# RWKV-7 scan of a diffusion trunk: its main loop laid out by hand over four units instead of by the scheduler's priorities

## The chip, the cores and the metric

One core of one Trainium2 chip runs the whole program, in fp32. The metric is the time of one execution in device microseconds (us), and lower is better.

## The reference

The program is a trunk of two layers over 512 latent tokens and 256 context tokens of width 1024. Each layer is half a SwiGLU, a token mixer, and half a SwiGLU; layer 0 mixes with HGRN2, layer 1 with RWKV-7. Only the scan of RWKV-7 is touched. Per head (16 of width 64) and per direction it computes

```python
def step(s, inp):
    dec, kt, vt, kkt, bt = inp[:5]
    sa = jnp.einsum('bhvk,bhk->bhv', s, kkt)
    s = s * dec[:, :, None, :] - sa[..., None] * bt[:, :, None, :] + vt[..., None] * kt[:, :, None, :]
    y = jnp.einsum('bhvk,bhk->bhv', s, inp[5]) if with_out else None
    return s, y
```

once over the context, whose final state starts the latent scan, and then over the latents, forward and backward; the two outputs are added, normed per head, gated and projected.

## The kernel before

The scan (`rwkv_scan`) works in chunks of 64 tokens. Twelve units (`todo`) are done one after the other: four groups of four heads (`qd`), and in each one unit of context (`g` = 0) and two of latents (`g` = 1, 2). A unit holds both directions (`d`), two head pairs (`e`), two heads to a pair (`hp`) and four chunks (`c`). Its steps, each a generator that yields between pieces:

- `prep_a`: loads hw, KR and ld (lines 1247, 1258, 1261) through SP's queue; decays on TensorE and ACT (sw, cum; tiles sg, E, Ei); scaled keys KR and BK on DVE (lines 1295, 1298); the products A on TensorE (line 1321) and their masked copies N and Ar on DVE (line 1327); the transpose NT (line 1332); and 16 small stores of 16x16 blocks, eight of N and eight of NT, to the DRAM tensor md (line 1335).
- `prep_m`: loads md as M (line 1347) and inverts all blocks on POOL in 14 pairs of small operations (lines 1353, 1354), then stores M to the DRAM tensor me (line 1357, from POOL's queue).
- `prep_d`: 16 small loads of me into X (line 1368).
- `prep_b`: loads VU (line 1377); turns BK into BKT (`bkt`, evicted by ACT at line 1386); products kT and W into KW.
- `prep_c`: transposes X on DVE (line 1409), merges the 16-blocks to 32 and 64 (T16, t16, R16, A32, AT32, TT, Yo, Y: lines 1421 to 1462), then four products YK (line 1472) whose evictions write KW and VU (lines 1473 to 1478), and four products P whose evictions write KR (lines 1486 to 1493).
- `scan`: four steps of the state G (lines 1519 to 1525) and, for latents, two outputs y (lines 1535 to 1545).
- `readout`: norm and gate of a head group's output, after its third unit.

The main loop takes one unit per turn. It emits the scan of unit i with pieces of the inversions, of the preparation of unit i+1 (`prep_b`, `prep_c`, `prep_d`) and of `prep_a` of unit i+2, at rates `RM`, `RP` and `RO`; the scheduler then orders each engine's and each queue's instructions by its own estimate of time, with a raised priority for three of the generators (`urgent`, `HP`). So the order on TensorE, DVE, ACT, POOL and SP is what the scheduler made of it. The PSUM banks of tags "a" (A, sw, cum) and "b" (bkt, kT, W, T16, R16, TT, Yo, YK, P) are two each, and X, VU, M, md and me have two buffers each.

Of the kernel before, what the change touches and what calls it, by code (L numbers as in the profile page):

```python
# [9 lines left out]
F32 = mybir.dt.float32  # L10
# [3 lines left out]
ALU = mybir.AluOpType  # L14
# [12 lines left out]
RINGS, NQ2, NG = {"KR": 6, "BK": 3, "Ar": 4}, 10, 5  # L27
# [44 lines left out]
def trunk(ctx, tc, io, phases=None, dump=None):  # L72
# [1109 lines left out]
    def rwkv_scan(l):  # L1182
# [11 lines left out]
        def Q(name):  # L1194
            if name not in RINGS:
                if "B2" in late:
                    if name == "N":
                        return late["B2"].tile([128, 1024], F32, tag="N", name=name, bufs=4)
                    return late["B2"].tile([128, 1024], F32, tag="Q", name=name, bufs=NQ2)
                ring = "Ar" if name == "N" else "KR"  # L1200
            else:
                ring = name
            return B1.tile([128, 1024], F32, tag=ring, name=name, bufs=RINGS[ring])
# [36 lines left out]
        def prep_a(qd, g):  # L1240
# [8 lines left out]
            gt = B1.tile([128, 4, 4], F32, tag="gt", name="gt", bufs=3)  # L1249
            gs = decays[qd, g] = B1.tile([128, 4], F32, tag="gs", name="gs", bufs=3)  # L1250
            lds, sgs, EEs = [], [], []
            for d in range(2):
                t0 = starts(g)[d]
                kr = Q("KR")[:, :1024]
# [4 lines left out]
                ld = B1.tile([128, 2, 2, 256], F32, tag="L", name="ld", bufs=2)  # L1259
# [52 lines left out]
            for d in range(2):  # L1312
# [4 lines left out]
                for e in range(2):  # L1317
                    for hp in range(2):
                        p = bank("A", "a")
                        for c in range(4):  # L1320
                            pe.matmul(p[:, 128 * c:128 * c + cols], BK[d][half(hp), 4 * e + c].rearrange("p s n -> p (s n)"),  # L1321
                                      KR[d][half(hp), 4 * e + c][:, :1 + lat], start=True, stop=True)
                        pv = p.rearrange("p (c s n) -> p c s n", s=2, n=64)
# [5 lines left out]
                        yield  # L1329
# [10 lines left out]
        def prep_m(qd, g):  # L1340
# [6 lines left out]
            nc.sync.dma_start(out=M, in_=md)  # L1347
# [13 lines left out]
        def prep_d(qd, g):  # L1361
            while (qd, g) not in inverse:
                yield
# [6 lines left out]
        def prep_b(qd, g):  # L1370
            KR, BK, N, Ar, gt, _ = ready[qd, g]
            BKT = [None, None]
            VU = late["B2"].tile([128, 2, 4, 2, 2, 64], F32, tag="VU", name="VU", bufs=2)
            for d in range(2):
                t0 = starts(g)[d]
                for hp in range(2):
                    nc.sync.dma_start(out=VU[half(1 - hp), d, :, hp].rearrange("p c e n -> p c (e n)"),
                                      in_=S["v"][t0:t0 + 256, hp, 128 * qd:128 * qd + 128].rearrange("(c p) n -> p c n", p=64))

            for d in range(2):  # L1380
# [7 lines left out]

            KW = [Q("KW").rearrange("p (e c x n) -> p e c x n", e=2, c=4, x=2) for _ in range(2)]
            for d in range(2):  # L1390
# [10 lines left out]
            ready[qd, g] = KR, N, Ar, BKT, VU, KW, gt  # L1401

        def prep_c(qd, g):
# [14 lines left out]
            for d in range(2):  # L1418
# [3 lines left out]
                yield  # L1422
            dve.tensor_tensor(t16.rearrange("p d s n -> p (d s) n"), p.rearrange("p d s n -> p (d s) n"), off16.unsqueeze(1).to_broadcast([128, 16, 32]), ALU.mult)
            p = view(bank("R16"))
            for d in range(2):
# [3 lines left out]
                yield  # L1429
# [9 lines left out]
            for stage in range(2):  # L1439
                for c in range(8):  # L1440
# [9 lines left out]
                    if c % 4 == 3:  # L1450
                        yield
                if stage == 0:
                    act.activation(tt, pt[:, :256], AF.Copy)
            for d in range(2):
# [46 lines left out]
        def scan(qd, g, KR, Ar, BKT, VU, gt):  # L1501
# [10 lines left out]
            for i in range(4):  # L1512
# [14 lines left out]
                if lat and i % 2:  # L1527

                    p = bank("y", "s")
                    pv = p.rearrange("p (q d e n) -> p q d e n", q=2, d=2, e=2)  # L1530
                    two = [(q, d, e, hp) for q in range(2) for d, e in DE for hp in range(2)]
                    where = lambda q, d: (i - 1 + q, q) if d == 0 else (4 - i - 1 + 1 - q, 1 - q)
                    for n, (q, d, e, hp) in enumerate(two):
                        c, o = where(q, d)
                        pe.matmul(pv[half(hp), o, d, e], VU[:, d, c, hp, e], Ar[d][:, slot(hp, e, c)], start=n < 2, stop=True, skip_group_check=n > 1)
                    for n, (q, d, e, hp) in enumerate(two):
                        c, o = where(q, d)
                        pe.matmul(pv[half(hp), o, d, e], Gs[i - 1 + q][half(hp), 2 * d + e], KR[d][half(hp), 4 * e + c, 1], start=False, stop=True, skip_group_check=True)
                    for d in range(2):
                        t0 = starts(g)[d] + 64 * where(0 if d == 0 else 1, d)[0]  # L1540
                        dst = yb[:, :, t0:t0 + 128].rearrange("p e (q n) -> p q e n", q=2)
                        if g == 1:
                            act.activation(dst, pv[:, :, d], AF.Copy)
                        else:
                            dve.tensor_tensor(dst, dst, pv[:, :, d], ALU.add)
                    yield
            state["G"] = G
# [44 lines left out]
        none = out = iter(())  # L1592
        stage = lambda f, i: f(*todo[i]) if i < len(todo) else none
        second = prep_a(*todo[1])

        def prologue():
            yield from prep_a(*todo[0])
            yield from both(prep_m(*todo[0]), islice(second, NPRO))
# [5 lines left out]
        for _ in both(second, chain(prep_d(*todo[0]), prep_b(*todo[0]), prep_c(*todo[0]))):  # L1604
            pass
        inversions = chain(*(prep_m(*k) for k in todo[1:]))
        third = stage(prep_a, 2)
        next(third)
        for i, k in enumerate(todo):
            ahead, third = urgent(third, HP[1]), stage(prep_a, i + 3)  # L1610
            b, c, d = stage(prep_b, i + 1), urgent(stage(prep_c, i + 1), HP[2]), urgent(stage(prep_d, i + 1), HP[2])
            prep = chain(islice(third, 1), islice(ahead, 4), b, d, ahead, c)
            due = [0.0] * 3
            for _ in urgent(scan(*k, *ready.pop(k)), HP[0]):
                for n, (f, r) in enumerate(((inversions, RM), (prep, RP), (out, RO))):
                    due[n] += r
                    while due[n] >= 1.0:
                        due[n] -= 1.0
                        next(f, None)
            for _ in prep:  # L1620
                next(inversions, None)
# [194 lines left out]
```

## Time and profile before

| | us |
|---|---|
| median of 3 runs (4023.62 to 4033.61) | 4023.75 |
| the profiled execution | 4034.11 |
| its span | 4032.3 |
| TensorE busy in the span | 3604.5 |
| DVE busy | 2515.7 |
| from the first whole X (unit 1) to the last (unit 11) | 619.95 |
| TensorE busy in that stretch | 475.54 |

Busy times are unions of an engine's instructions. TensorE's are modelled from pipelined records, and an fp32 product appears as two records. "PEclk" is the granted clock of TensorE as a share of 2.4 GHz. An idle time names what ended it. The scan's loop runs from about 2860 to 3557 us of the span.

### The profile page before, as it was taken

What the parts mean: (1) busy time and instruction counts of PE and PEld (TensorE: products, weight loads), DVE (VectorE), ACT (ScalarE), POOL (GpSimd) and SP (SyncE); (2) the same over time, 40 slices, a digit from 0 to 9 for tenths busy, and PEclk for the clock granted to TensorE, in tenths of its full rate; (3) what the DMA queues carried; (4) which work ended last, traced back from release to release, by engine and by line L of the source; (5) the groups of instructions that cost most, each with busy time, mean ns of one, the idle gap of its engine ahead of it and who ended that gap; (6) DMA issues with size and microseconds to landing.
All of it is one profiled execution on the core that took longest, in us unless ns stands there. A gap on an engine that the chain in (4) does not pass through costs nothing.

```text
span 4032.3 us, 71742 instructions
## 1 busy us (share of the span) xinstructions
PE 3604.5 (89%) x29954; PEld 3178.6 (79%) x29954; DVE 2515.7 (62%) x4108; ACT 1346.4 (33%) x2080; POOL 1073.7 (27%) x999
## 2 busy tenths in 40 slices
PE   5999997999997999998999997899777877788998
PEld 3899996788885888887999985667666766677887
DVE  6666767556667766657766666673333434268886
ACT  4333333333233333224332333443212222234343
POOL 3222224333344321214212214321101111014332
PEclk9999998999998999998999998998877878788999
DMA  5332321311112334332232232466212212132332
GB/s 186 115 95 89 108 71 48 110 43 43 43 43 63 92 104 124 100 100 68 89 98 80 83 96 65 132 227 186 72 48 53 72 46 61 32 110 72 96 95 83
DMA packets 520546, 356.90 MB, mean 89 GB/s; under 512 B 86589, under 2 KB 494941, under 8 KB 520222
## 3 DMA queue, kind: packets, MB, share of 16 engines
q1 hardware_dynamic: 518494, 348.65, 28.8%
q8 instruction: 235, 3.85, 0.4%
q10 hardware_dynamic: 1152, 2.10, 0.2%
q0 software_dynamic: 576, 1.57, 0.1%
q14 instruction: 89, 0.73, 0.1%
HBM read 312.52 MB, written 39.72 MB: 87 GB/s over the span
## 4 chain that ended last, share of the span: by engine, by line
PE 35%; DVE 6%; DMA 3%; POOL 2%; SPq 2%; issue 2%; ACT 1%; DVEq 0%; POOLq 0%; ACTq 0%
PE po L605 8%; PE c L532 6%; PE a L532 4%; PE b L532 3%; PE k L220 2%; PE v L220 1%; PE bkt L293 1%; SPq L1368 1%; PE A L1321 1%; POOL M L1354 1%; POOL mt L1353 1%; SPq L1335 1%; PE YK L1472 1%; PE G L1519 1%; DMA M<-md 1%
## 5 line engine op out<-in xcount | busy, mean ns | idle before, releaser
L605 PE MATMUL po<-g,whi 128*128 128x512 f32 (+1 forms) x2464 | 593.3, 350 | 10.2 <-ACT g L209 10.2
L532 PE MATMUL c<-u,whi 128*128 128x386 f32 (+1 forms) x2112 | 524.1, 332 | 50.8 <-DVE uu L563 15.9
L524 ACT ACTIVATE whi<-raw 128x1024 fp32r<-128x1024 f32 x352 | 332.8, 950 | 571.8 <-PE po L605 314.2
L549 POOL TENSOR_TENSOR raw<-raw 128x512 f32<-128x512 f32 x88 | 124.1, 1410 | 1374.1 <-DMA raw<-in_ffn_w_in 1040.3
L605 PEld LDWEIGHTS po<-g,whi 128*128 128x128 f32 x2464 | 406.3, 190 | 84.6 <-issue 11.4
L525 DVE TENSOR_TENSOR wlo<-raw,whi 128x1024 fp32r<-128x1024 f32 x352 | 412.1, 1174 | 33.7 <-ACT whi L524 31.9
L532 PEld LDWEIGHTS c<-u,whi 128*128 128x128 f32 x2112 | 371.2, 191 | 78.4 <-ACT u L444 30.1
L532 PE MATMUL a<-u,whi 128*128 128x386 f32 (+1 forms) x1408 | 350.1, 333 | 22.8 <-DVE u L426 17.2
L605 PE MATMUL po<-g,wlo 128*128 128x512 f32 (+1 forms) x1232 | 367.0, 348 | 0.0
L609 DVE SCALAR_TENSOR_TENSOR h<-po,mod,h 128x512 f32<-128x512 f32 (+1 forms) x384 | 228.3, 628 | 194.3 <-PE po L605 194.2
L532 PE MATMUL b<-u,whi 128*128 128x386 f32 (+1 forms) x1408 | 343.4, 328 | 2.6 <-DVE u L447 1.4
L532 PE MATMUL c<-u,wlo 128*128 128x386 f32 (+1 forms) x1056 | 344.8, 327 | 0.0
L532 PEld LDWEIGHTS a<-u,whi 128*128 128x128 f32 x1408 | 254.2, 194 | 28.5 <-issue 18.4
L194 ACT ACTIVATE whi<-raw 128x1024 fp32r<-128x1024 f32 (+1 forms) x193 | 184.5, 959 | 264.4 <-PE c L532 108.5
L532 PEld LDWEIGHTS b<-u,whi 128*128 128x128 f32 x1408 | 246.0, 189 | 12.6 <-issue 6.6
L532 PE MATMUL a<-u,wlo 128*128 128x386 f32 (+1 forms) x704 | 234.2, 333 | 0.2 <-DVE wlo L525 0.2
L605 PEld LDWEIGHTS po<-g,wlo 128*128 128x128 f32 x1232 | 207.9, 190 | 29.8
L532 PE MATMUL b<-u,wlo 128*128 128x386 f32 (+1 forms) x704 | 229.1, 325 | 0.7 <-DVE wlo L525 0.7
L1353 POOL TENSOR_TENSOR mt<-M 128x14 f32<-128x14 f32 (+6 forms) x168 | 44.6, 265 | 644.8 <-DMA M<-md 632.6
L195 POOL TENSOR_TENSOR wlo<-raw,whi 128x1024 fp32r<-128x1024 f32 x48 | 127.1, 2650 | 301.0 <-ACT whi L194 273.0
L532 PEld LDWEIGHTS c<-u,wlo 128*128 128x128 f32 x1056 | 203.3, 193 | 0.0
L195 DVE TENSOR_TENSOR wlo<-raw,whi 128x768 fp32r<-128x768 f32 (+1 forms) x145 | 174.3, 1204 | 38.0 <-ACT whi L194 37.7
(366 smaller groups left out, 7322.9 us busy)
## 6 DMA issues: line engine op xcount, KB each, us to landing
raw<-in_ffn_w_in SPq DMA_DIRECT2D x176, 512.0 KB
raw<-in_mod_w SPq DMA_DIRECT2D x144, 512.0 KB
raw<-in_ffn_w_out SPq DMA_DIRECT2D x80, 384.0 KB
raw<-in_hgrn_w_in SPq DMA_DIRECT2D x40, 512.0 KB
raw<-in_ffn_w_out SPq DMA_DIRECT2D x28, 512.0 KB
raw<-in_w_rkv SPq DMA_DIRECT2D x24, 512.0 KB
ld<-s_bk SPq DMA_DIRECT2D x48, 256.0 KB
s_bk<-knb SPq DMA_DIRECT2D x32, 192.0 KB
```

Of the source, the lines that this page charges most:

```text
L194: act.activation(hi[:, :m], raw[:, :m], AF.Copy)
L195: slots["lo"].tensor_tensor(lo[:, :m], raw[:, :m], hi[:, :m].bitcast(F32), ALU.subtract)
L220: pe.matmul(p[:, q:q + t1 - t0], a[:, k, c0:c0 + 128], b[:, t0:t1], start=(k == 0 and i == 0), stop=(k == nk - 1 and i == 2))
L293: pe.matmul(p, x, ident, start=True, stop=True)
L524: act.activation(hi, x, AF.Copy)
L525: dve.tensor_tensor(lo, x, hi.bitcast(F32), ALU.subtract)
L532: pe.matmul(p[:, :q], a[:, c], x[k][:, b], start=first and k == 0 and i == 0, stop=k == 3 and i == 2, skip_group_check=not first)
L549: pool.tensor_tensor(S[:, lo], U[:, lo], U[:, hi], ALU.add)
L605: pe.matmul(p[v][:, :t1 - t0], wx[:, k, at:at + 128], x[:, e, t0:t1], start=k == 0 and i == 0, stop=k == nk - 1 and i == 2)
L609: dve.scalar_tensor_tensor(h[d][:, t0:t1], p[v][:, :t1 - t0], mods[l, sub, 2][:, d, v:v + 1], h[d][:, t0:t1], ALU.mult, ALU.add)
L1321: pe.matmul(p[:, 128 * c:128 * c + cols], BK[d][half(hp), 4 * e + c].rearrange("p s n -> p (s n)"), KR[d][half(hp), 4 * e + c][:, :1 + lat ...
L1353: eng.tensor_tensor(t, M[:, 0:j, j:j + 1].to_broadcast([128, j, n]), M[:, j:j + 1, j + 1:16].to_broadcast([128, j, n]), ALU.mult)
```

## The change

The generators are emitted by fixed places in each turn, and inside a `manual_schedule` block TensorE, DVE, ACT and SP keep the order of emission; POOL stays with the scheduler. Four units are in work in a turn: unit i is scanned, unit i+1 goes through `prep_b` and `prep_c`, unit i+2 finishes `prep_a` (its A, N, NT and md) and is inverted, with its BKT (`prep_t`), VU (`prep_v`) and X (`prep_d`) loaded ahead, and unit i+3 starts `prep_a`. The load of M goes from SP's queue to POOL's. The A products of the two heads of a pair alternate in two banks instead of filling one bank after the other. The outputs y come after the four steps of G. Buffers get rings by name (`RINGS1`, `RINGS2`), and before the loop the preparation of units 1 and 2 is carried further.

```diff
+RINGS1, RINGS2 = {"KR": 6, "BK": 3, "Ar": 4, "L": 2}, {"KS": 2, "N": 4, "BKT": 4, "KW": 2, "NT": 1}
...
                 for e in range(2):
+                    ps_ = [bank("A", "a") for _ in range(2)]
+                    for c in range(4):
+                        for hp in range(2):
+                            pe.matmul(ps_[hp][:, 128 * c:128 * c + cols], BK[d][half(hp), 4 * e + c].rearrange("p s n -> p (s n)"),
+                                      KR[d][half(hp), 4 * e + c][:, :1 + lat], start=True, stop=True)
                     for hp in range(2):
-                        p = bank("A", "a")
-                        for c in range(4):
-                            pe.matmul(p[:, 128 * c:128 * c + cols], BK[d][half(hp), 4 * e + c].rearrange("p s n -> p (s n)"),
-                                      KR[d][half(hp), 4 * e + c][:, :1 + lat], start=True, stop=True)
...
-            nc.sync.dma_start(out=M, in_=md)
+            pool.dma_start(out=M, in_=md)
...
+        def laid(*streams):
+
+            order = sorted((a + (b - a) * (k + 0.5) / n, i) for i, (f, n, a, b) in enumerate(streams) for k in range(n))
+            for _, i in order:
+                next(streams[i][0], None)
+            for f, *_ in streams:
+                for _ in f:
+                    pass
...
+        run(chain(prep_d(*todo[0]), prep_v(*todo[0]), prep_t(*todo[0])))
+        run(both(chain(units[1], prep_t(*todo[1])), chain(prep_b(*todo[0]), prep_c(*todo[0]))))
+        run(chain(prep_m(*todo[1]), prep_v(*todo[1]), islice(units[2], 15), prep_d(*todo[1])))
         for i, k in enumerate(todo):
-            ahead, third = urgent(third, HP[1]), stage(prep_a, i + 3)
-            b, c, d = stage(prep_b, i + 1), urgent(stage(prep_c, i + 1), HP[2]), urgent(stage(prep_d, i + 1), HP[2])
-            prep = chain(islice(third, 1), islice(ahead, 4), b, d, ahead, c)
-            due = [0.0] * 3
-            for _ in urgent(scan(*k, *ready.pop(k)), HP[0]):
-                for n, (f, r) in enumerate(((inversions, RM), (prep, RP), (out, RO))):
-                    due[n] += r
-                    while due[n] >= 1.0:
-                        due[n] -= 1.0
-                        next(f, None)
-            for _ in prep:
-                next(inversions, None)
+            stage = lambda f, n: f(*todo[i + n]) if i + n < len(todo) else iter(())
+            ahead = units[i + 3] if i + 3 < len(todo) else iter(())
+            c = stage(prep_c, 1)
+            y = scan(*k, *ready.pop(k))
+            with tc.manual_schedule(engines=ORDERED | {mybir.EngineType.SP}):
+                laid((y, 4, 0, 0.36), (islice(ahead, 1), 1, 0.1, 0.3),
+                     (stage(prep_b, 1), 2, 0, 0.3), (c, 5, 0.06, 0.44),
+                     (units[i + 2] if i + 2 < len(todo) else iter(()), 5, 0.02, 0.4), 
+                     (chain(stage(prep_t, 2), stage(prep_m, 2)), 4, 0.4, 0.62), (y, 2, 0.4, 0.8), (c, 4, 0.46, 0.7), (c, 5, 0.72, 0.99),
+                     (islice(ahead, 14), 14, 0.5, 1.0), (out, 16, 0.0, 0.98))
+                if k[1] == 2:
+                    out = readout(k[0], state["y"], to_dram)
+                run(chain(stage(prep_v, 2), stage(prep_d, 2)))
```

What moves is shown at two places. The first is DVE around the transposes of X, in a turn that scans latents. X is the unit whose merge is to begin; VU and KR are of the unit before it in the kernel before; N and Ar (from A), and NT further on, are of a later unit. Before:

```order
L1327 TENSOR_TENSOR N<-A,cst_21938 128x256
L1327 TENSOR_TENSOR Ar<-A,cst_21938 128x256
L1409 STREAM_TRANSPOSE X_0_21946<-X_0_21946 128x256
L1476 COPY VU<-YK 64x4x64 x2
L1409 STREAM_TRANSPOSE X_0_21946<-X_0_21946 128x256
L1476 COPY VU<-YK 64x4x64 x2
L1491 TENSOR_TENSOR KR<-P,unit 128x256
L1493 TENSOR_TENSOR KR<-P,KR 128x256
```

Now:

```order
L1327 TENSOR_TENSOR Ar<-A,cst_21938 128x256
L1416 STREAM_TRANSPOSE X_0_21946<-X_0_21946 128x256 x2
L1327 TENSOR_TENSOR N<-A,cst_21938 128x256
L1327 TENSOR_TENSOR Ar<-A,cst_21938 128x256
L1327 TENSOR_TENSOR N<-A,cst_21938 128x256
L1327 TENSOR_TENSOR Ar<-A,cst_21938 128x256
L1530 TENSOR_TENSOR G<-G,gt 128x256
L1429 TENSOR_TENSOR t_27417<-T_27418,cst_21938 128x512
```

Before, the previous unit's VU and KR stand behind the transposes of X, and NT comes only after all of these, four G and all N. Now VU and KR of the previous unit stand ahead of X, and what follows X at once is the merge of X (t) and the N of the next unit to be inverted. The same stretch of DVE, at NT:

```order
L1327 TENSOR_TENSOR N<-A,cst_21938 128x256
L1327 TENSOR_TENSOR Ar<-A,cst_21938 128x256
L1551 TENSOR_TENSOR ybuf<-ybuf,y 128x2x2x64 x2
L1332 STREAM_TRANSPOSE NT<-N 128x1024
L1467 COPY Y_21948<-Yo 32x8x32 x2
L1481 COPY VU<-YK 64x4x64
```

NT now stands ahead of Y and VU of the unit whose X came last, where it stood behind those of the unit before.

The second place is SP's queue between two X. Before:

```order
L1247 DMA hw_s<-s_hw 65x256 x2
L1261 DMA ld<-s_bk_20093 128x2x256 x2
L1335 DMA md<-NT 16x8x16 x8
L1347 DMA M<-md 128x256
L1368 DMA X_0_21946<-me 16x8x16 x16
L1335 DMA md<-N 16x8x16 x8
```

Now:

```order
L1257 DMA KR<-s_kk 128x2x256
L1257 DMA KR<-s_r 128x2x256
L1260 DMA L<-s_bk_20094 128x2x256 x2
L1335 DMA md<-N 16x8x16 x8
L1335 DMA md<-NT 16x8x16 x8
L1376 DMA VU<-s_v 64x4x128 x4
L1257 DMA KR<-s_kk 128x2x256
L1366 DMA X_1_21947<-me 16x8x16 x16
```

The load of M has left SP's queue, and between the stores of NT and the loads of X there stand the loads of VU of the same unit and one load of KR.

## Rows read from the trace of the kernel before

**Rows 1.** The page: span, TensorE and DVE busy; the granted clock in 40 slices.

```profile
span 4032.3 us, 71742 instructions
PE 3604.5 (89%) x29954; PEld 3178.6 (79%) x29954; DVE 2515.7 (62%) x4108; ACT 1346.4 (33%) x2080; POOL 1073.7 (27%) x999
...
PEclk9999998999998999998999998998877878788999
```

**Rows 2.** Busy time by stretch: loop, rest of it, last unit. Columns in the first row.

```profile
core 0: us, PE busy (x) PEld busy (x) DVE busy (x) ACT busy (x) POOL busy (x), PEclk, DMA share, GB/s
2873.85:3493.80 619.95, 475.54 (x9940) 414.48 (x9936) 230.29 (x589) 154.13 (x351) 79.89 (x300) 0.80 0.21 53
3494.30:3517.50 23.20, 23.20 (x544) 21.47 (x542) 5.46 (x14) 6.14 (x13) 0.00 (x0) 0.95 0.13 40
3517.50:3556.60 39.10, 34.51 (x820) 29.94 (x818) 12.02 (x34) 8.14 (x18) 0.00 (x0) 0.78 0.02 5
```

**Rows 3.** Waits, 2870 to 3540 us: us in total, times, longest us.

```profile
POOL mt L1353 <- DMA M<-md: 516.7, 10, 59.9
...
DVE X L1409 <- DMA X<-me: 123.5, 13, 13.2
...
PE YK L1472 <- DVE VU L1476: 75.7, 9, 16.1
...
PE P L1486 <- DVE VU L1476: 20.0, 4, 9.8
PE TT L1447 <- DVE AT L1432: 14.1, 10, 1.6
```

**Rows 4.** DVE in order of time, one period: start, us, instruction, idle before it.

```profile
2999.47 0.45 DVE L1409 STREAM_TRANSPOSE X<-X 128x256 f32<-128x256 f32 x1 [11.00 <-DMA X<-me]
...
3004.91 0.45 DVE L1409 STREAM_TRANSPOSE X<-X 128x256 f32<-128x256 f32 x1 [4.19 <-DMA md<-N]
...
3022.58 0.75 DVE L1545 TENSOR_TENSOR ybuf<-ybuf,y 128x256 f32<-128x256 f32 x2 [0.73 <-PE y L1538]
...
3030.57 1.24 DVE L1332 STREAM_TRANSPOSE NT<-N 128x1024 f32<-128x1024 f32 x1
...
3060.01 0.45 DVE L1409 STREAM_TRANSPOSE X<-X 128x256 f32<-128x256 f32 x1 [11.24 <-DMA X<-me]
3060.48 0.77 DVE L1476 COPY VU<-YK 64x256 f32<-64x256 f32 x2
3063.90 0.45 DVE L1409 STREAM_TRANSPOSE X<-X 128x256 f32<-128x256 f32 x1 [2.65 <-DMA md<-N]
```

**Rows 5.** SP's queue in the same period: start, us of issuing, instruction.

```profile
3033.50 4.56 SPq L1335 DMA_DIRECT2D md<-NT  x8
3038.16 0.89 SPq L1261 DMA_DIRECT2D ld<-s_bk  x2
3039.29 0.34 SPq L1347 DMA_DIRECT2D M<-md  x1
3054.96 7.42 SPq L1368 DMA_DIRECT2D X<-me  x16
```

**Rows 6.** POOL in the same period, first and last of one inversion.

```profile
3043.18 0.20 POOL L1353 TENSOR_TENSOR mt<-M 128x14 f32<-128x14 f32 x1 [50.05 <-DMA M<-md]
...
3052.92 0.58 POOL L1357 DMA_DIRECT2D me<-M  x1 [0.30 <-POOL M L1354]
```

**Rows 7.** POOL, the first inversion, before the loop.

```profile
2782.61 0.44 POOL L1353 TENSOR_TENSOR mt<-M 128x14 f32<-128x14 f32 x1 [58.50 <-DMA M<-md]
...
2789.78 1.16 POOL L1354 TENSOR_TENSOR M<-M,mt 128x54 f32<-128x54 f32 x1
...
2794.86 0.71 POOL L1357 DMA_DIRECT2D me<-M  x1 [0.31 <-POOL M L1354]
```

**Rows 8.** The chain of waits, two crossings from NT to M: start, us, what.

```profile
3089.08 1.16 DVE NT L1332
...
3097.72 2.12 DMA M<-md
...
3153.17 1.16 DVE NT L1332
...
3160.03 2.00 DMA M<-md
```

**Rows 9.** TensorE in order of time, a later period.

```profile
3076.48 1.16 PE L1321 MATMUL A<-KR,BK 64*128 64x128 f32 x16
...
3078.65 1.16 PE L1321 MATMUL A<-KR,BK 64*128 64x128 f32 x8
...
3089.05 1.68 PE L1421 MATMUL T<-X,N 32*32 32x32 f32 x128 [0.17 <-ACT KW L1399]
...
3091.81 0.75 PE L1428 MATMUL R<-X,t 32*32 32x32 f32 x64
3094.32 1.08 PE L1428 MATMUL R<-X,t 32*32 32x32 f32 x64 [1.75 <-issue]
```

**Rows 10.** Groups by line, 2873.85 to 3493.8 us: count, busy us, mean ns.

```profile
L1519 PE MATMUL G<-VU,BKT 128*64 128x64 f32 x606 | 51.5, 257 | 3.8 <-ACT VU L1478 3.8
...
L1397 PE MATMUL W<-VU,N 64*64 64x64 f32 x640 | 34.1, 228 | 0.0
...
L1395 PE MATMUL kT<-cst,KR 64*64 64x64 f32 x640 | 32.7, 226 | 0.7 <-ACT KW L1399 0.7
L1523 PE MATMUL G<-G,KR 64*64 64x64 f32 x528 | 30.9, 232 | 1.7 <-DVE G L1525 1.7
...
L1535 PE MATMUL y<-Ar,VU 128*64 128x64 f32 x390 | 27.5, 239 | 0.0
...
L1538 PE MATMUL y<-KR,G 64*64 64x64 f32 x384 | 19.0, 231 | 0.0
```

More of the change, by code (lines that the diff above doesn't have):

```diff
@@ L1194, in Q @@
         def Q(name):
[L1195 to L1203, printed above, removed]
+            if "B2" not in late:
+                name = {"N": "Ar", "NT": "L"}.get(name, name)
+            name = {"bvl": "N", "gl": "N", "q": "KW"}.get(name, name)
+            ring = RINGS2.get(name) if "B2" in late else None
+            return (late["B2"] if ring else B1).tile([128, 1024], F32, tag=name, name=name, bufs=ring or RINGS1[name])
         turn = cycle(range(NB))
@@ L1368, in prep_d, with prep_v @@
                 nc.sync.dma_start(out=X[r0:r0 + 16, d, d, :, o:o + 16], in_=me[l0:l0 + 8].rearrange("l s t -> s l t"))
[L1370 to L1373, printed above, removed]
+            yield
+        bkts, vus = {}, {}
+        def prep_v(qd, g):
+            VU = vus[qd, g] = late["B2"].tile([128, 2, 4, 2, 2, 64], F32, tag="VU", name="VU", bufs=2)
             for d in range(2):
@@ L1400, in prep_b @@
                 yield
-            ready[qd, g] = KR, N, Ar, BKT, VU, KW, gt
         def prep_c(qd, g):
@@ L1526, in scan @@
                     yield
[L1527 to L1546, printed above, removed]
@@ L1547, in scan @@
-            state["G"] = G
+            state["G"] = G
+            for i in (1, 3) if lat else ():
+                p = bank("y", "s")
+                pv = p.rearrange("p (q d e n) -> p q d e n", q=2, d=2, e=2)
+                two = [(q, d, e, hp) for q in range(2) for d, e in DE for hp in range(2)]
+                where = lambda q, d: (i - 1 + q, q) if d == 0 else (4 - i - 1 + 1 - q, 1 - q)
+                for n, (q, d, e, hp) in enumerate(two):
+                    c, o = where(q, d)
+                    pe.matmul(pv[half(hp), o, d, e], VU[:, d, c, hp, e], Ar[d][:, slot(hp, e, c)], start=n < 2, stop=True, skip_group_check=n > 1)
+                for n, (q, d, e, hp) in enumerate(two):
+                    c, o = where(q, d)
+                    pe.matmul(pv[half(hp), o, d, e], Gs[i - 1 + q][half(hp), 2 * d + e], KR[d][half(hp), 4 * e + c, 1], start=False, stop=True, skip_group_check=True)
+                for d in range(2):
+                    t0 = starts(g)[d] + 64 * where(0 if d == 0 else 1, d)[0]
+                    dst = yb[:, :, t0:t0 + 128].rearrange("p e (q n) -> p q e n", q=2)
+                    if g == 1:
+                        act.activation(dst, pv[:, :, d], AF.Copy)
+                    else:
+                        dve.tensor_tensor(dst, dst, pv[:, :, d], ALU.add)
+                yield
@@ L1591, in rwkv_scan, with run @@
         todo = [(qd, g) for qd in range(4) for g in range(3)]
-        none = out = iter(())
-        stage = lambda f, i: f(*todo[i]) if i < len(todo) else none
-        second = prep_a(*todo[1])
+        out = iter(())
+        def laid(*streams):
[5 more added lines that the diff above has]
+                    pass
+        def run(f, n=None):
+            for _ in islice(f, n):
+                pass
+        units = [prep_a(*k) for k in todo]
         def prologue():
-            yield from prep_a(*todo[0])
-            yield from both(prep_m(*todo[0]), islice(second, NPRO))
+            yield from units[0]
+            yield from both(prep_m(*todo[0]), islice(units[1], 10))
         together(value_steps(vpool, bank), (prologue(), RV))
```

39 lines of the change are left out of this document (17 added, 22 removed).

## The prediction

> **What bounds the kernel now.** I read the page first. TensorE is busy for 3604.5 of 4032.3 us and DVE for 2515.7, so TensorE looks like the bound, and its granted clock shows nines and a few eights nearly everywhere; sevens stand only in the slices that hold the scan [rows 1]. The share of the whole span therefore says little about the scan, and the windows come next. In the 619.95 us between the first whole X and the last, ten units are started, so one unit takes 62.0 us. TensorE is busy for 475.54 of these at a clock of 0.80, which is 47.6 us per unit, or 47.6 x 0.80 = 38.0 us at the full clock [rows 2]. Some 14 us per unit are idle, and the work that is there runs slowly.
>
> The waits say on what. DVE waits for X 123.5 us in 13 waits, about 12 us per unit, and TensorE waits for VU 75.7 + 20.0 us, about 10 per unit [rows 3]. The second is a consequence of the first: in DVE's timeline the transpose of X of unit u stands in the queue ahead of VU of unit u-1. X idles DVE for 11.24 us, and VU runs 0.02 us after it [rows 4]. Since DVE works in order, a late X holds back work that doesn't need it.
>
> Why is X late? Following the period gives a closed circle. The second transpose of X ends the wait at 3004.91; NT of the next unit but one ends at 3031.81, 26.9 us on; and the second X of the next unit comes 32.1 us after that, at 3063.90 [rows 4]. Inside these 32.1 us stand the 16 stores of md on SP and the load of M, issued at 3039.29 [rows 5], the inversion on POOL from 3043.18 to 3052.92 [rows 6], the store of me, and the 16 loads of X from 3054.96, issued in 7.42 us [rows 5]. POOL works 9.7 us per unit and waits 50.05 [rows 6]. So the period is a latency, not an engine's work: (a) from X to NT on DVE and TensorE, and (b) from NT through DRAM and POOL to X.
>
> **The change, part by part.**
>
> (b) *From NT to X.* From the end of NT to the issue of M took 7.5 us and 5.7 us in the two crossings in the chain [rows 8]; the stores remain, ld no longer stands between NT and M, and I take 6.0. The load of M moves to POOL's queue, which no row shows. Bounds: me's store, which POOL issues, takes 2.04 us from POOL to the first load of X [rows 5, 6], and SP's load took 3.9 us from issue to POOL's first operation, of which 2.0 to 2.1 in flight [rows 5, 6, 8]. I take 2.6, nearer to me, which is a transfer of the same size from the same queue. The inversion is unchanged: 9.74 us when DVE mostly idles [rows 6], 12.25 in its first pass [rows 7]; I take 10.5, nearer to the first, which is the loop's own. Then me 2.0 and X 9.0 (3054.96 to 3063.90 is 8.94 [rows 4, 5]). Sum 6.0 + 2.6 + 10.5 + 2.0 + 9.0 = 30.1, with bounds of 28.3 (5.7 + 2.0 + 9.7 + 2.0 + 8.9) and 34.8 (7.5 + 3.9 + 12.3 + 2.0 + 9.1).
>
> The loads of VU, KR and ld now stand on SP between the stores of NT and the loads of X. They fall into the 15 us in which SP waits for M, the inversion and me, so I cost them at nothing. If the inversion ended before them, each would cost what two loads of ld take to issue, 0.9 us [rows 5].
>
> The Trainium skill, "DMA: Bandwidth & Descriptors", § Issuing engine by pattern, speaks against the move: a plain transfer belongs on SP or ACT. No row prices M there; me's 2.04 us is the nearest, and by it the move costs nothing.
>
> (a) *From X to NT.* VU, KR, YK and P of the unit before are now ahead of X. Behind X stand only: two transposes (0.9 us), T16 (1.68 [rows 9]), one group A (1.16), one step of G, one kT and W, R16 (0.75 + 1.08), the second A (1.16), one y, its addition ybuf (0.75), and NT (1.24) [rows 4, 9]. A step of G is (51.5 + 30.9) / 40 = 2.1 us, one of 20 pairs kT and W (34.1 + 32.7) / 20 = 3.3, and one of 12 outputs y (27.5 + 19.0) / 12 = 3.9 [rows 10]. The sum at these means is 18.1. With these three at the full clock (x 0.80) and y only in two of three units it is about 14. I take 16, against 26.9 before.
>
> *The period.* 30.1 + 16 = 46.1, and 2 for a fixed order in which one engine's late piece holds the next, about one wait of TensorE on AT (1.4 us, 14.1 / 10 [rows 3]) and a half: **48 us** instead of 62.0. The bounds are 42 (28.3 + 14) and 53 (34.8 + 18.1). TensorE's 38.0 us at the full clock fit into 48 us if the clock is above 0.8; with more of its work dense that is likely, as the one dense stretch shows (23.20 us busy of 23.20 at 0.95 [rows 2]).
>
> *A in alternation.* Sixteen alternating records took 1.16 us, and eight in one bank the same 1.16 [rows 9]. Four groups of sixteen then take 4.6 us, against at most 9.3; since the scheduler already mixes some of them I count 3 us of TensorE. They lie inside the circle only where the A in (a) stand, where I have used 1.16 already, so nothing is added.
>
> *The y behind all G, the rings, and BKT made ahead* move TensorE's work in time but do not change it. They are covered as long as TensorE has idle time, and I cost them at nothing. If that cover is gone, the first rival is the price.
>
> *The end of the loop.* At the last X the kernel before works 23.2 us on what stood behind X before T16 of the last unit can begin [rows 2]. That work now stands ahead of X. I count 21 us, leaving some 2.5 for a last y. The 39.1 us of the last unit remain, and so does everything outside the scan.
>
> *Sum.* 10 x (62.0 - 48) + 21 = 161 us. The profiled execution took 4034.1, so 3873; it lies 10.4 above the median of the runs, 4023.75, and I take that off: **3863 us**.
>
> **The rivals.**
>
> *TensorE becomes the bound.* For it: it is busy for 77% of a period, and the clock of 0.78 in the last unit's chain is no better [rows 2]. 47.6 x 0.80 / 0.78 = 48.8, less 3 for A, at the busy share of that stretch (34.51 / 39.10 = 0.88) gives 52 us per unit: 10 x 10 + 21 = 121, so 3903 us. Against it: the clock has been higher wherever the work was denser. Chance 0.20.
>
> *POOL is slowed by a busier DVE.* In its first pass, beside DVE's work, an operation of POOL took 1.16 us and the inversion 12.25 instead of 9.74 [rows 6, 7]. With 12.25 and 3.9 for M the period is 51 us, and the time 4034.1 - 10.4 - (10 x 10.95 + 21) = 3893 us. Chance 0.12. The Trainium skill, "SBUF — State Buffer", § SBUF: two separate sides, gives such a mechanism: GpSimd and VectorE share a pair of ports that one holds for a whole instruction, and a load issued from GpSimd's queue can be held back as well. By that rule M is exposed too; the trace agrees as far as the one operation of 1.16 us goes.
>
> *The short circle.* If every piece of (a) and (b) sits at its lower bound, the period is 42: 10 x 19.6 + 21 = 217, so 3806 us. Chance 0.13.
>
> *Slower: the whole turn comes into the circle.* In order, NT waits for every piece that stands ahead of it on TensorE, and in the turns that load and norm a head group's output, for these loads too. If N and NT of the next unit end only behind the whole of a unit's merge and scan, as at the loop's end in 39.1 us [rows 2], the period is 39.1 + 30.1 = 69.2: 10 x 7.2 - 21 = 51 us lost, so 4075 us. It decides from the point where X to NT takes more than 62.0 - 30.1 = 31.9 us, twice my value. For it: nothing can slip past a late piece any more. Against it: the listed order puts NT ahead of Y and VU. Chance 0.08.
>
> *It doesn't do what it says.* POOL stays with the scheduler, and the order across turns is not fixed by the table. If the circle stays at 62, only the end gains: 0 to 21 us, so 4003 to 4024. Chance 0.07.
>
> **How the numbers follow.** The forecast has 0.40, and the rivals 0.20, 0.12, 0.13, 0.08 and 0.07. The range runs from 3805, the short circle, to 3935, which is the bound of 53 us (10 x 9 + 21 = 111, so 3913) with two more us per unit. It leaves out the last two rivals. About 12 us, 0.3%, can be told from no change. Faster 0.87 (the first four, and a part of the last), same 0.05, slower 0.08.
>
> **What would show it.** Right: the transposes of X recur every 46 to 50 us; DVE's wait for X shrinks or no longer ends TensorE's waits; the waits of YK and P on VU are gone; POOL's wait for M falls from 50 to about 37 us; the clock in the loop rises to 0.85 or above. An inversion of over 12 us shows the POOL rival; TensorE busy for 90% or more of the loop shows the TensorE rival. Wrong: X to NT over 25 us, TensorE waiting on DVE's N or on ACT in place of VU, or SP's queue full when me lands, so that X starts late.

## The result, and the profile after

The changed kernel takes 3897.47 us (median of 3 runs, 3896.33 to 3908.28) against 4023.75: a ratio of 0.9686, 95% interval 0.9652 to 0.9721. The forecast was 3863 with a range of 3805 to 3935. The direction and the range held, and part of the mechanism did; the gain was 126 us and not 161.

The page of the changed kernel, against [rows 1] (its profiled execution took 3908.28 us):

```profile
span 3906.5 us, 71705 instructions
PE 3545.2 (91%) x29954; PEld 3127.6 (80%) x29954; DVE 2506.8 (64%) x4108; ACT 1346.8 (34%) x2080; POOL 1093.3 (28%) x1011
...
PEclk9999999999999899999999999798988888789999
```

The same work is done, with the same number of instructions on TensorE and DVE, in 125.8 us less. The windows say where, against [rows 2]: the loop from the second transpose of X of unit 1 to that of unit 11, and what follows it.

```profile
core 0: us, PE busy (x) PEld busy (x) DVE busy (x) ACT busy (x) POOL busy (x), PEclk, DMA share, GB/s
2870.80:3402.90 532.10, 444.10 (x10231) 385.28 (x10235) 236.25 (x624) 157.41 (x352) 95.72 (x310) 0.83 0.25 63
3402.90:3906.50 503.60, 450.58 (x3587) 406.29 (x3577) 384.50 (x613) 200.24 (x300) 154.70 (x106) 0.94 0.29 91
```

With the same marks, the loop before ran from 2874.3 to 3494.2. So 3.5 us were won ahead of the loop, 619.9 - 532.1 = 87.8 in it, and 538.1 - 503.6 = 34.5 behind it, together 125.8. A unit takes 53.2 us instead of 62.0. TensorE is idle for 88 of the 532 us, where it was for 144 of 620, and its clock is 0.83 instead of 0.80. The windows are of one execution each; whole executions of the changed kernel differ by 12 us.

The waits in the loop, against [rows 3]: total, times, longest.

```profile
POOL M L1347 <- DMA md<-NT: 333.9, 9, 43.4
...
DVE VU L1481 <- ACT VU L1483: 101.5, 40, 5.2
...
DVE X L1416 <- DMA X<-me: 60.4, 17, 7.1
...
PE T L1428 <- DMA X<-me: 14.1, 13, 2.2
...
PE kT L1404 <- DVE KR L1496: 9.8, 1, 9.8
```

The waits of YK and P on VU, 96 us before, are gone; TensorE's largest wait in total is 14.1 us in 13 short ones. DVE still waits for X, half as long. Its largest wait is now for ACT, which evicts the other part of YK (22.6 us in the loop before); whether that is on the path was not tested.

One period of DVE, against [rows 4], shows both parts of the circle (X, then NT, then the next X):

```profile
3025.17 0.45 DVE L1416 STREAM_TRANSPOSE X<-X 128x256 f32<-128x256 f32 x1 [4.42 <-DMA X<-me]
...
3042.31 1.24 DVE L1332 STREAM_TRANSPOSE NT<-N 128x1024 f32<-128x1024 f32 x1
...
3083.48 0.45 DVE L1416 STREAM_TRANSPOSE X<-X 128x256 f32<-128x256 f32 x1 [1.25 <-DMA X<-me]
3087.61 0.45 DVE L1416 STREAM_TRANSPOSE X<-X 128x256 f32<-128x256 f32 x1 [3.69 <-DMA X<-me]
```

From the second X to the end of NT it is now 18.4 us instead of 26.9; but from there to the next second X it is 44.1 instead of 32.1. SP's queue in the same period says why, against [rows 5]:

```profile
3043.58 4.95 SPq L1335 DMA_DIRECT2D md<-NT  x8
...
3058.48 0.75 SPq L1246 DMA_DIRECT2D hw_s<-s_hw  x2
3068.94 0.90 SPq L1260 DMA_DIRECT2D L<-s_bk  x2
...
3074.12 0.55 SPq L1594 DMA_DIRECT2D s_yo<-ybuf  x1
3074.72 2.65 SPq L1376 DMA_DIRECT2D VU<-s_v  x4
3077.46 8.62 SPq L1366 DMA_DIRECT2D X<-me  x16
```

POOL issued the store of me at 3063.31, so X could have been loaded from about 3065.4. It was issued at 3077.46, since L, s_yo and VU stand ahead of it on SP. Here L waits 9.6 us for BK, which reads the tile that was in its buffer, and s_yo, a store, for the normed output (its rows name KR, which DVE does beside the last step of the norm); VU then follows at once. In other units VU waits, for the output y that last reads its buffer.

SP's waits of these three in the loop (total, times, longest):

```profile
SPq L1376 <- PE y L1541: 35.1, 6, 20.2
...
SPq L1260 <- DVE BK L1297: 19.3, 2, 9.6
SPq L1594 <- DVE KR L1496: 19.0, 2, 18.5
```

X is issued 7.9 to 14.7 us behind me in six of ten units, and 2.0 to 3.4 in the rest. In units 3, 6 and 9 it is VU that holds it; in 5, 8 and 11, when a head group's output is normed, it is L or s_yo.

### The profile page after: what moved, and what is told of

Its sections match the earlier page's. It is cut to its first block, busy times and chain, and to the rows that moved or that the text cites. A ratio compares the mean times of both kernels' runs of the same rounds, so it can differ in the third digit from the quotient of the medians.

```text
span 3906.5 us, 71705 instructions
## 1 busy us (share of the span) xinstructions
PE 3545.2 (91%) x29954; PEld 3127.6 (80%) x29954; DVE 2506.8 (64%) x4108; ACT 1346.8 (34%) x2080; POOL 1093.3 (28%) x1011
## 4 chain that ended last, share of the span: by engine, by line
PE 34%; DVE 7%; SPq 3%; DMA 3%; issue 2%; POOL 2%; ACT 1%; DVEq 0%; POOLq 0%; ACTq 0%
PE po L607 8%; PE c L534 6%; PE a L534 4%; PE b L534 3%; SPq L1366 2%; PE k L222 2%; PE v L222 1%; PE A L1320 1%; PE o L222 1%; PE bkt L295 1%; PE YK L1477 1%; DVE mx L960 1%; DVE wlo L527 1%; POOL M L1354 1%; POOL mt L1353 1%
## 5 line engine op out<-in xcount | busy, mean ns | idle before, releaser
L607 PE MATMUL po<-g,whi 128*128 128x512 f32 (+1 forms) x2464 | 592.4, 350 | 10.6 <-ACT g L211 10.2
L534 PEld LDWEIGHTS a<-u,whi 128*128 128x128 f32 x1408 | 253.1, 193 | 28.1 <-issue 18.4
L316 POOL TENSOR_TENSOR nsq<-nsq 128x768 f32<-128x768 f32 (+1 forms) x49 | 101.7, 2076 | 218.4 <-ACT nsq L314 195.5
```

The lines of the kernel that those rows point to most:

```text
L316: pool.tensor_tensor(sq[:, :n], acc[:, :n], sq[:, :n], ALU.add)
L534: pe.matmul(p[:, :q], a[:, c], x[k][:, b], start=first and k == 0 and i == 0, stop=k == 3 and i == 2, skip_group_check=not first)
L607: pe.matmul(p[v][:, :t1 - t0], wx[:, k, at:at + 128], x[:, e, t0:t1], start=k == 0 and i == 0, stop=k == nk - 1 and i == 2)
```

## The experiments

Ratios are to the kernel before on the same chip; the changed kernel's is 0.9686 (0.9652 to 0.9721). "The loop" is the stretch from unit 1's X to unit 11's, 532.1 us in the changed kernel. A label stands for the one kernel.

**x_first: X ahead of VU on SP.**

```diff
-                run(chain(stage(prep_v, 2), stage(prep_d, 2)))
+                run(chain(stage(prep_d, 2), stage(prep_v, 2)))
```

> The changed kernel with X loaded ahead of VU on SP at the end of each turn. In the changed kernel six of ten units load X 7 to 14 us after me has landed (60 us in all), since the four loads of VU stand ahead and wait for the output y that last reads their buffer. Theory 1, the period is still the circle through X: most of these 60 us go, 3840 to 3855 us. Theory 2, TensorE's work and its clock set the period and X only happens to come in time: no more than TensorE's own waits for X go, 14 us and 4 for the transposes behind them, and some low clock behind these gaps: 3865 to 3885 us. If the late VU then holds W instead: 3897 or more.

Measured 0.9754 (0.9739 to 0.9768), some 27 us slower than the changed kernel; the loop takes 552.9 us. (The expectation's 7 to 14 us count from the issue of me; X could follow that in 2.0.) The last case of the expectation came true, as its waits show:

```profile
PE W L1406 <- DMA VU<-s_v: 55.0, 11, 12.2
```

VU is needed early in the next turn, for W, and TensorE stands up to 12 us for it. The queue has two loads that are late, and one of them must come second.

**a_in_turn: the products A of the two heads one bank after the other.**

```diff
-                    for c in range(4):
-                        for hp in range(2):
+                    for hp in range(2):
+                        for c in range(4):
                             pe.matmul(ps_[hp][:, 128 * c:128 * c + cols], ...
```

> The changed kernel with the A products of a pair's two heads one bank after the other again, not alternating. The prediction counted 3 us of TensorE per unit for it, at most 4.6. Theory 2 (TensorE sets the period): 30 to 46 us slower, 3927 to 3943. Theory 1 (the circle): only the two groups that stand between X and NT count, 2 x 1.16 us per unit, 3910 to 3920. If alternation does nothing on the chip in this place: 3897.

Measured 0.9682 (0.9668 to 0.9697): no difference. TensorE is busy 458.4 us in the loop instead of 444.1, so alternating saves it 1.4 us per unit against this strict order, and that moves nothing. Against the kernel before, whose scheduler mixed the banks already, the A products fell only from 71.9 us in the loop to 68.4, not by the 3 us per unit that the prediction counted.

**m_on_sp: M loaded by SP again.**

```diff
-            pool.dma_start(out=M, in_=md)
+            nc.sync.dma_start(out=M, in_=md)
```

> The changed kernel with the load of M back on SP's queue, at the end of the turn's loads, ahead of VU and X. Theory 1 (the circle): M costs 0 to 1.3 us more per unit, as the prediction's bounds have it (2.6 against 3.9 us), and its wait for md holds the loads behind it: 3897 to 3925. Theory 2 (TensorE): no difference, 3890 to 3905. If a load from POOL's queue is the slower one: 3880 to 3890.

Measured 0.9705 (0.9690 to 0.9719): no difference that the intervals show, with a loop of 536.8 us. In units 5, 8 and 11 M stood behind the rest of SP's queue and X came 7 to 12 us later behind NT than in the changed kernel, but units 4, 6, 9 and 10 took 2.5 to 6.4 us less.

**bkt_twice: the bkt products done twice.**

```diff
-                    for c in range(4):
+                    for c in [0, 1, 2, 3] * 2:
                         turned(p[:, 128 * c:128 * c + 128], ...
```

> The changed kernel with each of the sixteen bkt products of a unit done twice into the same place, 4 x 1.3 us more on TensorE per unit between NT and X, work that nothing in the circle waits for directly. Theory 2 (TensorE sets the period): 10 x 5.2 = 52 us slower, 3940 to 3960. Theory 1 (the circle, whose stretch from NT to X runs on SP, DMA and POOL): 0 to 10 us where the inversion sets X, up to 31 if in six units the later y passes it on to VU and X: 3897 to 3928.

Measured 0.9704 (0.9688 to 0.9720), not to be told from the changed kernel, and the loop is no longer than without the extra work (the window's columns as above):

```profile
2879.00:3408.20 529.20, 452.27 (x10587) 400.51 (x10591) 235.34 (x625) 156.82 (x352) 88.66 (x310) 0.89 0.25 64
```

The group of these products in the loop of the changed kernel and here (count, busy us, mean ns, idle us before it and what ended most of that):

```profile
L295 PE MATMUL bkt<-cst,BK 128*128 128x128 f32 x320 | 52.0, 315 | 9.8 <-ACT Y L1465 9.6 <-DVE ybuf L1579 0.2
L295 PE MATMUL bkt<-cst,BK 128*128 128x128 f32 x640 | 85.6, 293 | 5.5 <-ACT Y L1465 5.2 <-DVE ybuf L1579 0.3
```

So TensorE's amount of work is not what sets the loop's length. The bkt products took 33.6 us more in it, but TensorE as a whole was busy only 8 us longer, at a granted clock of 0.89 and not 0.83. The zero is a balance, though. Units 3, 6 and 9 took 2.5 to 7.4 us longer: there VU waits longer for the later y, and X was issued 2.6 to 6.3 us later behind me, as the expectation allowed for. The others took 0.7 to 6.4 us less. In units 2, 4, 7 and 10 one reason is in the rows: the inversion took 9.9 to 10.7 us, to the store of me, instead of 12.0 to 12.4.

**y_early, vu_three, x_on_pool, sp_free: four ways to free SP's queue.**

```diff
y_early
-                     (y, 2, 0.4, 0.8),
+                     (y, 2, 0.36, 0.5),
vu_three
-            VU = vus[qd, g] = late["B2"].tile([128, 2, 4, 2, 2, 64], F32, tag="VU", name="VU", bufs=2)
+            VU = vus[qd, g] = late["B2"].tile([128, 2, 4, 2, 2, 64], F32, tag="VU", name="VU", bufs=3)
x_on_pool
-                nc.sync.dma_start(out=X[r0:r0 + 16, d, d, :, o:o + 16], ...
+                pool.dma_start(out=X[r0:r0 + 16, d, d, :, o:o + 16], ...
sp_free
-            with tc.manual_schedule(engines=ORDERED | {mybir.EngineType.SP}):
+            with tc.manual_schedule(engines=ORDERED):
```

> The changed kernel with the two outputs y placed right behind the last step of G (0.36 to 0.5 of the turn, not 0.4 to 0.8), so that VU's buffer is free earlier and SP can load VU and, behind it, X. Theory 3: period and lateness come from SP's queue, where VU waits for the y that last reads its buffer and X stands behind VU; x_first has shown that either of the two late costs time. Then X starts within 3 us of me in units 3, 6 and 9, the 14 us of waits of TensorE on X and some low clock behind them go: 15 to 30 us below the changed kernel, a ratio to before of 0.961 to 0.965. Rival: the two y standing earlier push T, A and NT back, and TensorE idles more late in the turn, which brings the clock down: ratio 0.969 to 0.975.

> The changed kernel with three buffers for VU (room for it from one buffer less for hw and for w2), so that VU's load waits for no y of its turn. Theory 3 (SP's queue): as y_early, 15 to 30 us, ratio 0.961 to 0.965; X stays late only in units 5, 8 and 11, behind the loads of L, bvl, gl and the store of s_yo. Rival, the loads behind hw and w2 now wait on sw: no gain, 0.969 to 0.973.

> The changed kernel with the 16 loads of X issued by POOL, right behind the store of me, so that nothing of SP's queue stands ahead of them. Theory 3: X is never late behind VU, L or s_yo; POOL issues one load in about 0.6 us like its other transfers, 16 x 0.6 + 2 = 12 us against 9 on SP: X comes 5 to 10 us earlier in six units and 3 later in four; 10 to 30 us gained, ratio 0.961 to 0.966. Rival, POOL's issue of small loads is slow, over 1 us each: X comes 16 us or more after me in all units, slower, 0.972 to 0.985.

> The changed kernel with SP left to the scheduler; TensorE, DVE and ACT keep the written order. Theory 3: what SP loses is in its written order (VU ahead of X, L and s_yo ahead of both), so the scheduler's order may give back up to 30 us or do worse by as much, since it doesn't know when a buffer comes free: 0.961 to 0.977. If the order on SP makes no difference: 0.967 to 0.970.

Measured 0.9661 (0.9641 to 0.9681), 0.9668 (0.9646 to 0.9689), 0.9669 (0.9654 to 0.9685) and 0.9678 (0.9663 to 0.9694), with loops of 532.8, 531.4, 520.5 and 531.8 us. None can be told from the changed kernel with these runs. The lateness went as it should: X is issued 2.6 to 4.7 us after me in every unit with x_on_pool, and 2.0 to 3.7 with sp_free. But in units 3, 5, 6, 8 and 9 of x_on_pool DVE came to X only 1 to 8 us after its last load was issued, where it otherwise waits for the loads. And in sp_free the way from NT to X shrank from 39.7 to 36.4 us per unit, while that from X to NT grew from 13.5 to 16.8. A late X was not the only thing that held these turns.

**half_in_before, half_in_after: half of the inversion left out** in units 2 to 11 (what these kernels compute is then not the reference's).

```diff
-                n = 15 - j
-                t = mt[:, :j * n].rearrange("l (a b) -> l a b", b=n)
+                if j % 2 == 0 and todo.index((qd, g)) > 1: yield; continue
+                n = 15 - j; t = mt[:, :j * n].rearrange("l (a b) -> l a b", b=n)
```

> The kernel before, with every second of the 14 steps of the inversion left out for units 2 to 11 (the output is not the reference's): POOL's 9.2 us become about 4.8. Theory of the prediction: the loop before is the circle from X through NT, md, M, the inversion and me to X, so each of ten periods shrinks by the same 4.4 us: 40 to 46 us less than before, ratio 0.989 to 0.990. Rival, the loop before is bound by an engine and X is only one of several late things: 0 to 15 us, 0.996 to 1.000. The scheduler also moves some instructions of the loop for the shorter inversion, which may add or take some us.

> The changed kernel with the same steps left out. If the circle still sets the period, as the prediction's sum has it: 10 x 4.5 = 45 us less than the changed kernel, ratio to before 0.956 to 0.959. Theory 4, the circle no longer binds since the other variants moved X by 10 us without a change of time, and the period is the turn itself, TensorE's work at its granted clock with short hops to ACT and DVE in between: 0 to 12 us less, 0.965 to 0.969.

In the changed kernel: 0.9620 (0.9600 to 0.9640), a loop of 505.6 us, 26.5 less, between the two expectations. The units tell why. The period of each unit, from the second transposes of X:

| unit | 2 | 3 | 4 | 5 | 6 | 7 | 8 | 9 | 10 | 11 |
|---|---|---|---|---|---|---|---|---|---|---|
| changed kernel | 56.0 | 46.6 | 52.3 | 62.4 | 45.2 | 51.6 | 63.1 | 44.0 | 54.7 | 56.2 |
| half_in_after | 48.7 | 51.9 | 47.7 | 63.0 | 43.6 | 44.0 | 60.0 | 46.6 | 45.1 | 55.1 |
| two_queues (below) | 54.5 | 41.3 | 49.0 | 56.6 | 45.0 | 50.3 | 54.4 | 44.3 | 50.5 | 49.0 |

Units 2, 4, 7 and 10, whose X waits for nothing on SP, gain 29 us, and their inversions, the four longest of the changed kernel, had shrunk by 27 (6.6 to 7.1 each); the other six, whose X stands behind SP's queue, lose 3. So the circle still binds where SP's queue is out of the way.

In the kernel before: 1.0017 (1.0001 to 1.0034), no gain. From NT to X it took 27.1 us instead of 31.3, as meant; but from X to NT 36.2 instead of 30.7. The scheduler had put X ahead of more of the previous unit's work. Its DVE in the period of [rows 4]:

```profile
2997.09 0.45 DVE L1409 STREAM_TRANSPOSE X<-X 128x256 f32<-128x256 f32 x1 [1.89 <-DMA X<-me]
2997.56 0.77 DVE L1476 COPY VU<-YK 64x256 f32<-64x256 f32 x2
3002.47 0.43 DVE L1476 COPY VU<-YK 64x256 f32<-64x256 f32 x1 [4.14 <-ACT VU L1478]
3005.88 0.43 DVE L1476 COPY VU<-YK 64x256 f32<-64x256 f32 x1 [2.98 <-ACT VU L1478]
3011.98 0.42 DVE L1491 TENSOR_TENSOR KR<-P,unit 128x256 f32<-128x256 f32 x1 [5.67 <-PE P L1489]
```

The clock in its loop was 0.77 instead of 0.80. Since the order changed with the edit, this run doesn't tell what a shorter circle is worth to the loop before at a fixed order. That stays open.

**warm_t: the first half of T done three times, to fill TensorE's waits for the second half of X.**

```diff
-            for d in range(2):
+            for d in (0, 0, 0, 1):
                 for c in range(8):
                     for hp, b, a in rows32:
                         pe.matmul(p[a:a + 32, d, c], N[d]...
```

> The changed kernel with the first half of the products T done three times into the same place, which fills TensorE's waits of some 1.8 us for the second half of X (seven of ten units) with 1.7 us of repeated work. Theory 4, second part: a gap of TensorE of one to three us is followed by a stretch of 7 to 17 us at the low clock, which costs more than the gap; bkt_twice did 39 us more work at a clock of 0.89 instead of 0.83 in the same time. Then filling these gaps removes four to six such stretches: clock in the loop 0.86 or above and 10 to 25 us less, ratio 0.961 to 0.966. Rival, the clock falls for other reasons than these gaps: the repeated work only adds to the units that don't wait, 0 to 10 us more, 0.968 to 0.971.

Measured 0.9724 (0.9709 to 0.9740), some 15 us slower, though the intervals still touch; a loop of 551 us, at the same clock:

```profile
2872.50:3423.50 551.00, 455.73 (x11592) 396.70 (x11592) 236.79 (x625) 157.47 (x352) 94.70 (x310) 0.83 0.24 62
```

The gaps before T were not filled. T's group in the two loops, the changed kernel's first:

```profile
L1428 PE MATMUL T<-X,N 32*32 32x32 f32 x1395 | 23.5, 214 | 17.9 <-DMA X<-me 14.1 <-DVE X L1416 3.7
L1428 PE MATMUL T<-X,N 32*32 32x32 f32 x2756 | 37.0, 207 | 31.1 <-issue 29.1 <-DVE X L1416 1.8
```

The waits for X's loads are gone by name, but TensorE stands idle before T for 31.1 us instead of 17.9, now for nothing that the profile names ("issue"). So whether short gaps before T bring the clock down is not tested by this run. What it shows is where the path runs: with the longer T, X to NT took 16.1 us per unit instead of 13.5, NT to X 0.7 less, and the unit 1.9 more. A delay of TensorE between X and NT lengthens the loop; one between NT and X (bkt_twice) did so in the context units alone, and not on balance.

**two_queues: X on POOL's queue, and half of NT's stores too.** x_on_pool's edit, and

```diff
             for d, hp, b, l0, r0 in lanes:
-                nc.sync.dma_start(out=md[l0:l0 + 8].rearrange("l s t -> s l t"),
+                (pool if d and hp else nc.sync).dma_start(out=md[l0:l0 + 8].rearrange("l s t -> s l t"),
```

> The changed kernel with all loads of X on POOL's queue, as x_on_pool, and also half of the eight stores of NT to md, so that SP and POOL store NT side by side. Reading of the runs so far: the work done twice on TensorE between NT and X cost nothing (bkt_twice, loop 529 against 532 us), the work repeated between X and NT cost its whole time (warm_t, 1.7 us per unit, loop 551), and 4.6 us less of inversion gave 26 us in the loop, all in the four units whose X waited for nothing on SP. So the circle still binds in part of the units. If that is right, x_on_pool's 12 us in the loop stay and 2 us more go in each latent unit: loop 500 to 515 us, ratio to before 0.961 to 0.965. Rival, the turn's written order binds as soon as X is in time (x_on_pool had X waiting 2 to 8 us for DVE in five units): nothing beyond x_on_pool, loop 518 to 524, ratio 0.965 to 0.968.

Measured 3876.02 us against 4034.95, 0.9605 (0.9591 to 0.9618), clear of the changed kernel's interval: the fastest version here, some 33 us below the change and a little below what the expectation gave the circle.

```profile
2872.90:3367.70 494.80, 418.89 (x10114) 363.31 (x10116) 235.13 (x624) 157.03 (x352) 195.18 (x510) 0.89 0.27 68
```

Its queues store NT side by side, four each, on SP:

```profile
2986.07 1.73 SPq L1335 DMA_DIRECT2D md<-NT  x4
```

and on POOL, with the load of M behind:

```profile
2986.33 2.09 POOL L1335 DMA_DIRECT2D md<-NT  x4 [28.47 <-DVE NT L1332]
2990.36 0.57 POOL L1347 DMA_DIRECT2D M<-md  x1 [1.94 <-DMA md<-NT]
```

In the table above, units 5, 8 and 11 gain 22 us (X no longer behind L and s_yo), units 2, 4, 7 and 10 gain 10 (the shorter way from NT to X), and units 3, 6 and 9 gain 5. The clock in the loop is also 0.89, against 0.85 with X alone on POOL's queue (x_on_pool, a loop of 520.5 us). How much of the gain the clock gave is not separated.

## Why the prediction was right, and where its size was off

**The mechanism.** That VU and KR of the previous unit would stand ahead of X and TensorE's waits on VU would go came true in the waits. That X to NT shrinks came true: 13.5 us on average from the end of X's transposes, against the forecast's 16 and 30.7 before. But the average is partly luck. It is 17.8 where NT belongs to a latent unit, above the forecast, and 3.4 where it belongs to a context unit, whose A comes ahead of X, which the list of what stands behind X did not foresee. That the circle is what the new loop runs on is shown in part, by half_in_after, warm_t and two_queues. That it was the one bound of the loop before is not shown: half_in_before didn't bear it out. Nor did a run change the kernel before in one part alone, so how the gain divides over the parts of the change is argued from the waits; only for M's place and the alternation of A do runs show that they give nothing that can be told.

**The term that was mis-sized** is (b), from NT to X: 30.1 forecast, 39.7 measured, above the bound of 34.8.

| from NT to X, us per unit | forecast | measured |
|---|---|---|
| end of NT to issue of M | 6.0 | 7.5 |
| M to POOL's first operation | 2.6 | 3.1 |
| inversion, to the store of me | 10.5 | 10.8 |
| me to the first load of X | 2.0 | 7.3 |
| loads of X, to the second transpose | 9.0 | 10.6 |

(The 0.45 us of the transpose itself complete the 39.7.) The step that failed is the sentence that "the loads of VU, KR and ld now stand on SP between the stores of NT and the loads of X" and cost nothing. Their issue costs little; but in six of ten units one of them (ld is L in the new kernel), or the store s_yo, which the sentence did not name, waits for a buffer or for its data, and X stands behind that wait: 5.3 of the 9.6 us. I had priced the transfers and not what they wait for. So a unit took 39.7 + 13.5 = 53.2 us instead of 48, and the loop gave 88 us and not 140. The total hid part of that miss: 13.5 us more than forecast came at the end and 3.5 ahead of the loop.

Yet curing SP alone gave at most 12 us in the loop (x_on_pool), and none with sp_free, where X to NT grew in its place. So (a) and (b) are not two independent terms, as the sum took them: when X comes earlier, other work in the turn's order holds DVE. Which piece it is stays open.

**The signs.** Of those of being right, the waits on VU are gone and POOL's wait for M is 37.1 us (333.9 / 9); but X recurs every 44 to 63 us, not 46 to 50, and the clock is 0.83, below 0.85. One sign of being wrong came true, SP's queue full when me lands. The POOL rival's sign came true in four of ten units, TensorE's did not: it is busy for 83% of the loop.

**Readings that were off.** NT of the circle is of the next unit, not the next but one. Only the eight stores of NT stand between NT and M; the eight of N are issued elsewhere [rows 5]. The pieces of (a) with three of them at the full clock add up to about 15 us, not 14. And the clock was not higher wherever the work was denser: the last unit's stretch is busier than the loop (0.88 against 0.77) at a lower clock (0.78 against 0.80) [rows 2].

**The end.** 21 us forecast, 34.5 measured. The last y ended 62.4 us behind the last X before and 35.1 now. Another 10.2 us went between that y and the last norm's mean. TensorE's rows of the kernel before (start, us, instruction), where it stands behind the norm of the other half:

```profile
3565.84 2.08 PE L293 MATMUL rsb<-cst,q 128*128 128x128 f32 x8 [5.42 <-ACT q L1568]
3567.71 3.81 PE L1559 MATMUL mean<-ybuf,cst 128*128 128x512 f32 x4
```

In the changed kernel it follows y at once:

```profile
3436.87 1.15 PE L1544 MATMUL y<-KS,G 64*64 64x64 f32 x32
3438.87 1.98 PE L1564 MATMUL mean<-ybuf,cst 128*128 128x512 f32 x4 [0.85 <-DVE ybuf L1551]
```

What follows gave 3.0 us back. The prediction had not looked at the norm.

**The rivals.** TensorE as the bound: not borne out by bkt_twice, though its 3903 us were near the measured time; the agreement is chance. POOL slowed by DVE: true in part. Counted to the store of me, as the prediction did, the inversion took 12.0 to 12.4 us in units 2, 4, 7 and 10 and 9.8 to 10.0 in the rest. Its 3893 us are the nearest of all, but by luck: it put 12.25 us in every unit and 3.9 for M, where the averages are 10.8 and 3.1. One of those over 12 us in order of time (start, us, instruction), POOL's rows first:

```profile
3005.45 0.29 POOL L1353 TENSOR_TENSOR mt<-M 128x56 f32<-128x56 f32 x1
3005.82 0.73 POOL L1354 TENSOR_TENSOR M<-M,mt 128x56 f32<-128x56 f32 x1
...
3008.74 0.60 POOL L1354 TENSOR_TENSOR M<-M,mt 128x44 f32<-128x44 f32 x1
3009.42 0.25 POOL L1353 TENSOR_TENSOR mt<-M 128x36 f32<-128x36 f32 x1
```

And DVE's at the same time:

```profile
3005.69 0.69 DVE L1294 TENSOR_TENSOR KR<-KR,E 128x512 f32<-128x512 f32 x1
...
3008.46 0.75 DVE L1297 TENSOR_TENSOR BK<-L,Ei 128x512 f32<-128x512 f32 x1
3009.24 0.42 DVE L1496 TENSOR_TENSOR KS<-P,unit 128x256 f32<-128x256 f32 x1
```

POOL's operation beside KR<-KR,E and the one beside BK<-L,Ei, which read two tiles of SBUF, took 0.73 and 0.60 us; the one beside KS<-P, which reads P from PSUM, took 0.25, and like sizes alone some 0.3. The Trainium skill, "SBUF — State Buffer", § SBUF: two separate sides, says just this: a VectorE operation with two inputs in SBUF and a GpSimd operation that reads SBUF exclude each other for a whole instruction. The trace agrees: the two long operations end 0.13 to 0.17 us behind DVE's. It is worth 4 x 2.3 = 9 us here. The short circle, the turn's whole serial path (slower) and no effect did not occur. The rule of "DMA: Bandwidth & Descriptors", § Issuing engine by pattern, also of the Trainium skill, that plain transfers belong on SP or ACT, was not borne out here: M's place made no difference that the intervals show (m_on_sp), and X and half of NT's stores on POOL's queue were the best version.

## What to carry to other kernels

In a queue that works in program order, price a moved transfer by what it waits for, not by its issue: everything behind it inherits the wait. When a loop is a circle through memory, add work at two places to see where the path runs, before any engine is called the bound; and read the answer unit by unit, for a total of nothing can be a gain and a loss (bkt_twice), and work that is meant to fill a gap may only move it (warm_t). And shorten the circle where its small transfers are issued one by one: an idle engine's queue took half of them.

## What the runs showed of the hardware

- An addition to TensorE's work can come with a higher clock: in bkt_twice 33.6 us more of bkt products in the loop made TensorE 8 us busier there, at a granted clock of 0.89 instead of 0.83. In warm_t, with 13.5 us more of T, it stayed at 0.83. What tells the two apart is not settled.
- POOL's queue issues a small load in about 0.53 us (X, eight in 4.21 us in two_queues), about as fast as SP (sixteen in 7.42 us [rows 5], and in 7.4 to 9.8 in the changed kernel's loop):

```profile
3005.73 4.21 POOL L1366 DMA_DIRECT2D X<-me  x8 [2.00 <-PE P L1491]
```
